# The input's transpose as a product with diag(1/rms), and tokens 256 to 511 first

## The chip, the core and the metric

The kernel runs on one core of one Trainium2 chip. A core has a matrix engine (TensorE, PE in the profile, with its weight loads as PEld), a vector engine (VectorE, DVE), a scalar engine (ScalarE, ACT), a general engine (GpSimd, POOL) and a queue engine that only issues transfers (SyncE, SP). Each works through its own list of instructions in order; semaphores tie the lists together. The metric is the time of one execution in microseconds on the device.

## What is computed

One layer over 512 tokens of width 2048, with 16 learned meta tokens ahead of them. The opening that the change touches is the first two lines of the layer: the norm, and the projection by `w_in`.

```python
def rms_norm(x, gain):
    y = x * lax.rsqrt(jnp.mean(x * x, axis=-1, keepdims=True) + EPS)
    return y * gain

def hybrid_layer(x, ...):                     # x: meta tokens, then tokens
    h = rms_norm(x, norm_g)
    proj = h @ w_in                           # 2048 x 12368
    q_a, k_a, v_a, z_a, q_i, k_i, w_i, q_b, f_b, i_b, z_b, gates = split(proj)
    o_a = dsa_attention(...)                  # indexer scores, top-128 keys, attention
    o_b = hgrn2_chunkwise(...)                # gated recurrence in chunks of 64
    y = stack([o_a * silu(z_a), rms_norm(o_b) * silu(z_b)])
    p = einsum('btnc,ncd->btnd', y, w_branch)
    return x + sum(sigmoid(gates) * p, axis=2) @ w_out
```

All data are float32.

## The kernel before

**Layout.** The projections need h with channels on partitions, in 16 tiles of 128 channels (`kt` 0 to 15) by 528 tokens: columns 0 to 15 are the meta tokens, then four blocks of 128 tokens, numbered 0 to 3. x comes with tokens on partitions, four pieces of 512 channels for each block (`load_x`, tiles `x` in the profile; `xm` for the meta tokens, two tiles of 1024 channels). The meta tokens and blocks 0 and 1 make half 0 (272 columns), blocks 2 and 3 half 1 (256 columns).

**Precision.** Every large product runs on the fast type fp32r in three matmuls. An operand is held as a rounded part and a remainder: `hH` and `hL` for the input, `eh`/`el` or `wh`/`wl` for weights out of the loaded `raw` tiles. ACT writes the rounded part, DVE (for some early weights POOL) the remainder. `mm3` issues high by high, high by low and low by high.

**The opening, step by step.** `norm_x(b)` is a generator: sums of squares of two pieces on ACT and two on DVE (two yields), then the mean and the power -1/2 on POOL (one yield; the factor 1/rms lies in `st[b][:, 6]`), then four scalings of x in place by that factor on DVE, one for each piece, with a yield behind each. `prep(half, kt)` transposes the scaled pieces of its blocks for tile kt into one PSUM bank `px` (`E.tr`, line 102), and then ACT (`hH`) and DVE (`hL`) read the bank with the norm's gain as scale. The main loop runs half 0 and then half 1; in each it goes over kt, first calls `prep` two tiles ahead, then issues six projection matmuls into `pg`: three for 80 columns of the indexer's keys and weights, three for the first 128 columns of its queries. `FIRST` says in which order the norm's steps of the first blocks are written out before the loop, `NEXT` at which (half, kt) the other steps stand, `SPLITS` where weight chunks are split. `fill` issues transposes of the identity into a spare bank `pw`: 33 before the first `prep`, and four in each of the first three steps.

**Transfers.** SP issues, in this order, x of block 0, meta, x of block 1, four weight chunks, x of blocks 2 and 3, further weight chunks. The x tiles are slots of a pool and go back to it behind their last transpose; meta lies in two weight buffers.

**Behind the opening.** Classifying jobs follow (512-column matmuls `pg`: the indexer's queries, then four gate pieces; `jobs[2:]`), then pairs of column blocks by a Strassen scheme with seven products (`px`, `py`, `pz`, `pv`, `pw` from `hH`, `hL` and the sums `tT`). The sums are made by `tops_task` on DVE and ACT while the classifying jobs run; `place_t3` then overwrites half of `hH`/`hL` with one of them. Indexer scores, top-k (`topk_task`: on DVE, 16 rounds of maximum and replace for each of four blocks of queries), the mask tables, HGRN and attention are tasks (generators) too.

**What sets the order.** The program is written out by a planner on the host. `Core` keeps a modelled clock for each engine. `pump(limit)` lets tasks take a step when their inputs are due and the modelled DVE and ACT clocks are less than `limit` ahead of PE's. `finish(t)` takes steps of all tasks without a limit until t is done. At the last classifying job (`ji == nclass`) `finish(t_task[0])` is called, so that `tops_task` is written out whole before the job's matmuls. Tiles that find too few free slots (`hold`) are stored to memory (`held`) and fetched again.

Of the kernel before, what the change touches and what calls it, by code (L numbers as in the profile page):

```python
# [8 lines left out]
F32 = mybir.dt.float32  # L9
# [9 lines left out]
NM = 16  # L19
# [10 lines left out]
KQ = (144, 272, 400, 528)  # L30
WAIT = object()

FIRST = ((0, 2), ("m", 2), (0, 1), ("m", 1), (1, 3), (0, 1), ("m", 1), (1, 1))
NEXT = {(0, 0): (1,), (0, 2): (0, "m", 1), (0, 5): (0, "m", 1), (0, 6): (2,), (0, 7): (2,), (0, 8): (3,),
        (0, 9): (2, 3), (0, 10): (2, 3), (0, 11): (3,), (0, 13): (3,), (0, 15): (2, 3), (1, 2): (2, 3),
        (1, 6): (2,)}
SPLITS = {(0, 3): 2, (0, 4): 3, (1, 9): 4, (1, 12): 5}
LAT = 180.0
SAME = {"pe": 0.0, "act": 60.0, "dve": 125.0, "pool": 60.0}
MARGIN = 300.0  # L40
NZA = 4
FILL = 4
NSLOT = 71
ORDER = (1, 0)
NC_, ND_ = 1, 0
# [143 lines left out]
def hybrid_kernel(ctx, tc, x, meta, vecs, w_in, rows, w_branch, w_out,  # L189
# [15 lines left out]
    class Task:  # L205
# [3 lines left out]
        def step(self):  # L209
            try:  # L210
                r = next(self.gen)
            except StopIteration:
                self.done = True
                tasks.remove(self)
                return True
            if r is WAIT:
                return False
            self.t = r or 0.0
            return True
# [21 lines left out]
    def finish(t):  # L241
        z = 0
        while not t.done:
# [9 lines left out]
            else:  # L253
                any(u.step() for u in list(tasks)) or stuck("fin")

    need = [2]

    def bank(name):
# [15 lines left out]
    def slots(name, n=1, dt=F32):  # L274
        return [S.get(name, dt) for _ in range(n)]
# [5 lines left out]
    def ready(*aps):  # L281
        return max(E.ac.get(a.tensor.name, (0.0, ""))[0] for a in aps) + LAT

    X = {}
    blocks = [("m", NM, 0)] + [(b, 128, NM + 128 * b) for b in range(4)]

    def load_x(b, q):
        X[b] = slots("x", 4)
        for c in range(4):
            q.dma_start(X[b][c][:, :512], x[0, 128 * b:128 * b + 128, 512 * c:512 * c + 512])  # L290

# [1 line left out]
    E.dve([mhalf], [], 8, lambda v: v.memset(mhalf, -0.5))  # L293
    warm = cp.tile([128, 1], F32, name="warm")
    E.act(warm, mhalf[:, 0:1], AF.Square)
    load_x(0, nc.sync)
    ident = cp.tile([128, 128], F32, name="ident")
    nc.gpsimd.dma_start(ident, ident_d)
    vrow = cp.tile([35, 128], F32, name="vrow")
    nc.gpsimd.dma_start(vrow, vecs)  # L300
    X["m"] = []
    for c in range(2):
        s = wp.tile([128, 1024], F32, name=f"xm{c}", tag=f"wh{c}")
        nc.sync.dma_start(s[:NM, :], meta[:, 1024 * c:1024 * c + 1024])
        X["m"] += [s[:, 0:512], s[:, 512:1024]]
    load_x(1, nc.sync)
    RB = cp.tile([128, 192], F32, name="RB")
    tabA = cp.tile([128, 5, 64], F32, name="tabA")
    tabI = cp.tile([128, 5, 32], F32, name="tabI")
# [79 lines left out]
    def split_upto(i):  # L389
        while state["split"] <= min(i, len(preps_) - 1):  # L390
            k = state["split"]
            ch = preps_[k]
            if "pair" in ch:
                prep_op(k, ch)
            else:
                split_chunk(k, ch)
            state["split"] += 1
# [100 lines left out]

    st = {b: cp.tile([128, 8], F32, name=f"st{b}") for b, _, _ in blocks}
    junk = slots("junk", 2)  # L500

    def norm_x(b):
        p = NM if b == "m" else 128
        for c in range(4):
            xs, ac = X[b][c][:p, :512], st[b][:p, c:c + 1]
            if c % 2:
                E.dve([junk[c % 2], st[b]], [xs], 512, lambda v: v.scalar_tensor_tensor(
                    junk[c % 2][:p, :512], xs, 1.0, xs, op0=OP.mult, op1=OP.mult, accum_out=ac))
            else:
                E.act(junk[c % 2][:p, :512], xs, AF.Square, accum_out=ac)  # L510
            if c % 2:
                yield
        E.red(st[b][:p, 4:5], st[b][:p, 0:4])
        E.ts(st[b][:p, 5:6], st[b][:p, 4:5], 1.0 / D, EPS, OP.mult, OP.add)
        E.ptt(st[b][:p, 6:7], st[b][:p, 5:6], mhalf[:p, 0:1], OP.pow)
        yield
        for c in range(4):
            xs = X[b][c][:p, :512]
            E.ts(xs, xs, st[b][:p, 6:7], None, OP.mult)
            yield  # L520

    hH, hL = [], []

    def prep(half, kt):
        if half == 0:
            hH.append(slot("hH", F32R))
            hL.append(slot("hL", F32R))
        bs = ((("m", 0, 1)), (2, 3))[half]
        pb = B1.get("px")
        o = 0  # L530
        for b in bs:
            p = NM if b == "m" else 128
            E.tr(pb[:, o:o + p], X[b][kt // 4][:p, 128 * (kt % 4):128 * (kt % 4) + 128], ident[:p, :p])
            o += p
        c = slice(272 * half, 272 * half + o)
        g = cvec[:, kt:kt + 1]
        E.act(hH[kt][:, c], pb[:, :o], AF.Copy, scale=g)
        E.stt(hL[kt][:, c], pb[:, :o], g, hH[kt][:, c].bitcast(F32), OP.mult, OP.subtract)
        B1.put(pb)
        if kt % 4 == 3:  # L540
            S.put(*[X[b][kt // 4] for b in bs if b != "m"])
# [1261 lines left out]
    stream[1], stream[2] = stream[2], stream[1]  # L1803
    preps_[1], preps_[2] = preps_[2], preps_[1]
    load_upto(3)
    load_x(2, nc.sync)
    load_x(3, nc.sync)
    load_upto(NRAW - 1)
    pb = B1.get("pc")
    E.tr(pb[:, :35], vrow, ident[:35, :35])  # L1810
# [10 lines left out]
        for _ in range(n):  # L1821
            next(gens[b], None)

    for b, n in FIRST[:4]:
        step(b, n)
    E.act(cvec, pb[:, :35], AF.Copy)
    B1.put(pb)
    for b, n in FIRST[4:]:
        step(b, n)
    split_upto(0)  # L1830
    prep(0, 0)
    split_upto(1)
    step(0)
    step("m")
    kb, qb = B2.get("pg"), B1.get("pg")
    preps = iter([(i, kt) for i in range(2) for kt in range(KT)][1:])

    def prep_next():
        p = next(preps, None)
# [1 line left out]
            prep(*p)  # L1841

    prep_next()
    for half in range(2):
        n = (272, 256)[half]
        for kt in range(KT):
            prep_next()
            if half == 0 and kt < 3:
                fill(FILL)
            elif half == 0 and kt == 3:  # L1850
                B1.put(pw)
            for ji in range(2):
                if ji == 0:
                    c = slice(272 * half, 272 * half + n)
                    o = kb[:80, half, :n]
                else:
                    c = slice(16 + 256 * half, 272 + 256 * half)
                    o = qb[:, 256 * half:256 * half + 256]
                mm3(o, jobs[ji].chunks[kt // 8], kt % 8, kt, hH[kt][:, c], hL[kt][:, c], kt == 0, kt == KT - 1)
            for b in NEXT.get((half, kt), ()):  # L1860
                step(b)
            if (half, kt) in SPLITS:
                split_upto(SPLITS[half, kt])
            if (half, kt) == (1, 8):
                load_consts()
    jobs[0].done(kb)
    jobs[1].done(qb)
    S.put(*junk, *early)
    for k in E.clk:
        E.clk[k] = max(E.clk[k], E.clk["pe"]) + (2500.0 if k in ("dve", "act") else 0.0)  # L1870
    npair, late = 0, []
# [1 line left out]
    for ji, job in enumerate(jobs[2:], 3):  # L1873
        need[0] = 1 + jobs[ji].meta if ji < len(jobs) else 0
        if job.pre:
            job.pre()
        if job.req:
            job.req()
        if job.kind == "pair":
            npair += 1  # L1880
            last = npair == npairs
            run_pair(job, jobs[ji] if isinstance(jobs[ji], Pair) else None, late, last)
            continue
        if job.kind == "br" and isinstance(job, Pair):
            finish(t_y)
            run_br(job, jobs[ji] if isinstance(jobs[ji], Pair) else None, job.c0 // 256, job.unit)
            continue
        if job.kind == "out":
            if ji - 1 == first_out:
                OB.extend(B1.get("po") for _ in range(6))  # L1890
                OB.append(B2.get("po")[:, 0])
                load_xq(0)
            nxt = jobs[ji] if ji < len(jobs) else None
            run_out(job, nxt)
            continue
        z = 0
        while len(B1.free) < 1 + job.meta:
            z += 1
            if z > 3000:
                stuck("job")  # L1900
            pump(1e9)
            if len(B1.free) < 1 + job.meta:
                E.clk["pe"] += 200
        if job.meta:
            b = [B1.get("pg"), B1.get("pg")]
            parts = [(b[c][:, :264], slice(264 * c, 264 * c + 264)) for c in range(2)]
        else:
            b = B1.get("pg")
            parts = [(b[:job.ncols, :], slice(16, 528) if job.kind == "in" else slice(0, 512))]
        if ji == nclass:  # L1910
            finish(t_task[0])
        for ch in job.chunks:
            split_upto(ch["prep"] + 2)
            flush()
            for kk_ in range(ch["nk"]):
                kt = ch["k0"] + kk_
                if job.kind == "in":
                    mh, ml = hH[kt], hL[kt]
                else:
                    mh, ml = yH[job.n, kt], yL[job.n, kt]  # L1920
                for o, c in parts:
                    mm3(o, ch, kk_, kt, mh[:, c], ml[:, c], kt == 0, kt == job.kts - 1)
                pump(500.0 if ji == nclass else 3000.0)
            if ji == nclass and ch["k0"] == 0:
                place_t3(0)
                place_t3(4)
        job.done(b)
# [72 lines left out]
```

## Time and profile before

| | us |
|---|---|
| median of 3 runs (lowest, highest) | 1530.59 (1528.6, 1531.83) |
| the profiled execution, its own time | 1529.07 |
| span of that profile | 1527.3 |
| first matmul on PE | 7.91 |
| first projection matmul (`pg`) | 15.98 |
| first 512-column projection matmul | 51.33 |
| first Strassen matmul | 195.55 |

A row of the timeline reads: start, duration, engine, line of the kernel, operation, result<-operands by the names in the kernel, shapes, count. A count x2 or more merges instructions that follow each other, and the duration then runs from the first start to the last end. In square brackets stands how long the engine sat idle before, and what ended that. A matmul's duration holds its way through the array, so matmuls overlap; what one costs is read from the distance of starts. Groups give busy time, mean nanoseconds of one, and the idle time before them. A stretch's row gives its bounds and length, then busy time and count of PE, PEld, DVE, ACT and POOL, the granted clock, the share of the DMA engines and GB/s.

### The profile page before, as it was taken

Reading aid. Unit: us, or ns where it says so; the run is one execution under the profiler, and the core shown is the slowest. Engines: PE = TensorE matmul, PEld = TensorE weight load, DVE = VectorE, ACT = ScalarE, POOL = GpSimd, SP = SyncE. Lnnn points to the kernel's source line nnn. Section 1 sums busy time; section 2 is a strip of 40 time slices with the busy share of each in tenths; the row PEclk is TensorE's granted clock in tenths of the full one; section 3 lists DMA queues with packets and bytes.
Section 4 is the critical chain, followed back from the end, with each engine's and each line's share of the span. In section 5 each row is a group of like instructions: output and inputs, shape, how many; then the busy total and the mean of one; then the engine's idle time right before and its main releaser. Section 6 shows DMA issues by size and latency. Waiting matters only on the chain.

```text
span 1527.3 us, 31296 instructions
## 1 busy us (share of the span) xinstructions
PE 1500.9 (98%) x12756; PEld 1435.2 (94%) x12756; DVE 1201.0 (79%) x2013; ACT 712.5 (47%) x1079; POOL 165.9 (11%) x180
## 2 busy tenths in 40 slices
PE   7999999999999999999999999999999999999998
PEld 6888889999999999999999999999999799989998
DVE  6699899999977787787768768768756768898765
ACT  5565444444434444434554554554454544444342
POOL 2100010010001001011101101101010000002221
PEclk9999999999999999999999999999999999999999
DMA  9323448766666585758677677676678767748883
GB/s 266 83 70 83 110 103 196 187 168 166 162 172 164 148 190 137 185 131 198 142 192 181 156 192 180 161 191 166 164 203 195 228 188 188 212 123 217 214 214 90
DMA packets 300288, 256.50 MB, mean 168 GB/s; under 512 B 11828, under 2 KB 262208, under 8 KB 300144
## 3 DMA queue, kind: packets, MB, share of 16 engines
q1 hardware_dynamic: 271392, 177.44, 40.0%
q0 software_dynamic: 15616, 56.71, 21.3%
q10 hardware_dynamic: 13136, 20.35, 4.2%
q8 instruction: 100, 1.64, 0.5%
q14 instruction: 44, 0.36, 0.1%
HBM read 169.11 MB, written 28.73 MB: 130 GB/s over the span
## 4 chain that ended last, share of the span: by engine, by line
PE 86%; DVE 8%; DMA 2%; issue 2%; ACT 2%; ACTq 0%; SPq 0%; POOL 0%; DVEq 0%
PE pz L96 16%; PE px L96 16%; PE pg L98 12%; PE po L96 10%; PE pv L96 8%; PE pw L96 8%; PE py L96 8%; DVE wl L112 2%; PE phl L98 1%; PE pov L96 1%; PE psc L98 1%; PE plg L98 1%; PE pho L98 1%; ACT wh L106 1%; DVE tk L697 1%
## 5 line engine op out<-in xcount | busy, mean ns | idle before, releaser
L106 ACT ACTIVATE wh<-raw 128x1024 fp32r<-128x1024 f32 x416 | 440.1, 1059 | 557.7 <-PE pz L96 148.9
L112 DVE TENSOR_TENSOR wl<-raw,wh 128x1024 fp32r<-128x1024 f32 x414 | 508.3, 1228 | 148.1 <-ACT wh L106 144.7
L121 POOL DMA_DIRECT2D raw<-raw x108 | 95.0, 993 | 969.0 <-DVE raw L112 678.3
L96 PE MATMUL px<-hH,wh 128*128 128x272 f32 (+1 forms) x672 | 194.6, 290 | 1.3 <-ACT p L106 1.3
L96 PE MATMUL px<-hL,wh 128*128 128x272 f32 (+1 forms) x672 | 192.1, 286 | 0.0
L96 PE MATMUL px<-hH,wl 128*128 128x272 f32 (+1 forms) x672 | 192.1, 286 | 0.0
L96 PE MATMUL po<-wh,mh 128*128 128x256 f32 x896 | 158.5, 281 | 0.5 <-DVE xq L112 0.5
L96 PEld LDWEIGHTS po<-wh,mh 128*128 128x128 f32 x896 | 137.3, 189 | 0.8 <-DVE xq L112 0.7
L112 DVE TENSOR_TENSOR raw<-raw,raw 128x1024 f32<-128x1024 f32 x108 | 132.0, 1222 | 1.8
L96 PEld LDWEIGHTS px<-hH,wh 128*128 128x128 f32 x672 | 126.9, 189 | 2.1 <-ACT p L106 1.6
L96 PEld LDWEIGHTS px<-hL,wh 128*128 128x128 f32 x672 | 126.9, 189 | 0.0
L96 PEld LDWEIGHTS px<-hH,wl 128*128 128x128 f32 x672 | 126.8, 189 | 0.0
L96 PE MATMUL pw<-tT,wh 128*128 128x256 f32 x672 | 126.4, 287 | 0.0
L96 PE MATMUL po<-wl,mh 128*128 128x256 f32 x448 | 125.7, 280 | 0.0
L96 PE MATMUL pv<-tT,wh 128*128 128x256 f32 x672 | 125.1, 285 | 0.0
L96 PE MATMUL pz<-tT,wh 128*128 128x256 f32 x672 | 124.3, 284 | 0.2 <-ACT wh L106 0.2
L96 PEld LDWEIGHTS pz<-tT,wh 128*128 128x128 f32 x672 | 103.2, 189 | 0.9 <-ACT wh L106 0.4
L96 PEld LDWEIGHTS pv<-tT,wh 128*128 128x128 f32 x672 | 103.0, 189 | 0.5
L96 PEld LDWEIGHTS pw<-tT,wh 128*128 128x128 f32 x672 | 103.1, 189 | 0.2
L96 PE MATMUL pz<-hH,wh 128*128 128x256 f32 x336 | 97.3, 289 | 2.9 <-DVE r L112 2.9
L96 PE MATMUL py<-hH,wl 128*128 128x256 f32 x336 | 94.8, 282 | 1.9 <-DVE wl L112 1.9
L96 PE MATMUL py<-hH,wh 128*128 128x256 f32 x336 | 95.9, 286 | 0.0
(349 smaller groups left out, 3582.9 us busy)
## 6 DMA issues: line engine op xcount, KB each, us to landing
raw<-in_w_in_dram SPq DMA_DIRECT2D x192, 512.0 KB, 6.1
raw<-raw POOLq DMA_DIRECT2D x108, 512.0 KB, 6.0
raw<-in_w_branch_dram SPq DMA_DIRECT2D x32, 512.0 KB, 6.3
raw<-in_w_out_dram SPq DMA_DIRECT2D x32, 512.0 KB, 6.5
gd<-r SPq DMA_DIRECT2D x32, 256.0 KB, 2.0
gate<-gd SPq DMA_DIRECT2D x32, 256.0 KB, 6.2
held<-r SPq DMA_DIRECT2D x19, 264.0 KB, 4.0
held<-r SPq DMA_DIRECT2D x18, 256.0 KB, 2.0
```

The lines of the kernel that those rows point to most:

```text
L96: self.nc.tensor.matmul(out, lhsT, rhs, start=start, stop=stop, skip_group_check=True)
L98: self.nc.tensor.matmul(out, lhsT, rhs, start=start, stop=stop)
L106: self.nc.scalar.activation(out, in_, f, **kw)
L112: self.nc.vector.tensor_tensor(out, a, b, op=op)
L121: self.nc.gpsimd.dma_start(out, a, accum_op=OP.add)
L697: e = E.dve([w], [src, m8], kq, lambda v: v.match_replace(w, m8, src, NEG))
```

## The change

The norm's factor is no longer multiplied into x. `norm_x` ends with one instruction that multiplies the identity by the block's factors, which gives the diagonal matrix `DG[b]` (128x128, for meta 16x16, in one new slot `dg`), and `prep` multiplies the unscaled x by it: the transpose `E.tr` becomes an ordinary float32 matmul with x as stationary and `DG[b]` as moving operand. The halves change places: the loop runs half 1 first (blocks 2 and 3, no meta), then half 0 (meta, 0, 1). Block 2 and 3 are loaded first; meta and blocks 0 and 1 behind the first four weight chunks. `FIRST` and `NEXT` follow. At the last classifying job `alone` takes the place of `finish`: it steps only `tops_task`, and lets other tasks step, up to 1500 ns ahead (`FLOOD`), only where that one is blocked.

```diff
-FIRST = ((0, 2), ("m", 2), (0, 1), ("m", 1), (1, 3), (0, 1), ("m", 1), (1, 1))
-NEXT = {(0, 0): (1,), (0, 2): (0, "m", 1), (0, 5): (0, "m", 1), (0, 6): (2,), (0, 7): (2,), (0, 8): (3,),
...
+FIRST = ((2, 3), (3, 2), (2, 1), (3, 2))
+NEXT = {(0, 4): ("m",), (0, 5): ("m",), (0, 6): (0,), (0, 7): (0,), (0, 8): (1,), (0, 9): (0, 1), (0, 10): (0, 1), (0, 11): (1, "m"),
...
+FLOOD = 1500.0
...
+    def alone(t):
+
+        z = 0
+        while not t.done:
+            z += 1
+            if z > 3000:
+                stuck("alone")
+            if t.t > E.clk["pe"]:
+                E.clk["pe"] = t.t
+            elif not t.step():
+                pump(FLOOD)
+                E.clk["pe"] += 200
...
-    load_x(0, nc.sync)
+    load_x(2, nc.sync)
...
-    X["m"] = []
-    for c in range(2):
-        s = wp.tile([128, 1024], F32, name=f"xm{c}", tag=f"wh{c}")
-        nc.sync.dma_start(s[:NM, :], meta[:, 1024 * c:1024 * c + 1024])
-        X["m"] += [s[:, 0:512], s[:, 512:1024]]
-    load_x(1, nc.sync)
+    load_x(3, nc.sync)
...
+    dg, DG = slot("dg"), {}
...
-        for c in range(4):
-            xs = X[b][c][:p, :512]
-            E.ts(xs, xs, st[b][:p, 6:7], None, OP.mult)
-            yield
+        DG[b] = dg[:p, 512:512 + NM] if b == "m" else dg[:, 128 * b:128 * b + 128]
+        E.ts(DG[b], ident[:p, :p], st[b][:p, 6:7], None, OP.mult)
+        yield
...
-        if half == 0:
+        if len(hH) <= kt:
...
-            E.tr(pb[:, o:o + p], X[b][kt // 4][:p, 128 * (kt % 4):128 * (kt % 4) + 128], ident[:p, :p])
+            E.mm(pb[:, o:o + p], X[b][kt // 4][:p, 128 * (kt % 4):128 * (kt % 4) + 128], DG[b], True, True)
...
     load_upto(3)
-    load_x(2, nc.sync)
-    load_x(3, nc.sync)
+    X["m"] = []
+    for c in range(2):
+        s = wp.tile([128, 1024], F32, name=f"xm{c}", tag=("wh0", "wl0")[c])
+        nc.sync.dma_start(s[:NM, :], meta_t[:, 1024 * c:1024 * c + 1024])
+        X["m"] += [s[:, 0:512], s[:, 512:1024]]
+    load_x(0, nc.sync)
+    load_x(1, nc.sync)
     load_upto(NRAW - 1)
...
-    prep(0, 0)
+    prep(1, 0)
     split_upto(1)
-    step(0)
-    step("m")
     kb, qb = B2.get("pg"), B1.get("pg")
-    preps = iter([(i, kt) for i in range(2) for kt in range(KT)][1:])
+    preps = iter([(i, kt) for i in (1, 0) for kt in range(KT)][1:])
...
-    for half in range(2):
+    for turn, half in enumerate((1, 0)):
...
-    S.put(*junk, *early)
+    S.put(*junk, *early, dg)
...
         if ji == nclass:
-            finish(t_task[0])
+            alone(t_task[0])
```

How this moves instructions shows at three places.

On PE, behind the 33 warming transposes, before the change (`px` is the bank that `prep` fills, `x_73` a piece of block 0, `x_89` of block 1, `xm` meta, `pw` the fillers):

```order
L102 MATMUL pw_196<-ident 128x128 x33
L102 MATMUL px_267<-ident,xm_85 128x16
L102 MATMUL px_267<-ident,x_73 128x128
L102 MATMUL px_267<-ident,x_89 128x128
...
L102 MATMUL px_299<-ident,x_89 128x128
L102 MATMUL pw_196<-ident 128x128 x4
L98 MATMUL pg_287<-hH_265,eh_255 80x272
```

The same place with the change (`x_73` is now a piece of block 2, `x_85` of block 3):

```order
L102 MATMUL pw_197<-ident 128x128 x33
L98 MATMUL px_260<-dg_109,x_73 128x128
L98 MATMUL px_260<-dg_109,x_85 128x128
...
L98 MATMUL px_288<-dg_109,x_85 128x128
L102 MATMUL pw_197<-ident 128x128 x4
L98 MATMUL pg_277<-hH_258,eh_248 80x256
```

The transposes have become products of x and `dg`, and in the first turn two stand for a tile and not three; the six projection matmuls of a step are as many as before.

On SP, the first transfers from the fourth on, before the change:

```order
L290 DMA x_76<-in_x_dram 128x512
L304 DMA xm_85<-in_meta_dram 16x1024
L304 DMA xm_87<-in_meta_dram 16x1024
L290 DMA x_89<-in_x_dram 128x512
L290 DMA x_90<-in_x_dram 128x512
L290 DMA x_91<-in_x_dram 128x512
L290 DMA x_92<-in_x_dram 128x512
L381 DMA raw_166<-in_w_in_dram 128x8x80
```

And with it:

```order
L303 DMA x_76<-in_x_dram 128x512
L303 DMA x_85<-in_x_dram 128x512
L303 DMA x_86<-in_x_dram 128x512
L303 DMA x_87<-in_x_dram 128x512
L303 DMA x_88<-in_x_dram 128x512
L389 DMA raw_163<-in_w_in_dram 128x8x80
```

The second block of x and the first weights move ahead by the two transfers of meta.

On DVE, at the last classifying job, before the change (`tr` and `tT` are steps of `tops_task`, MAX and MATCH_REPLACE a round of top-k, `masks` the mask tables, `wl` the remainder of the first Strassen weight):

```order
L112 TENSOR_TENSOR tr_2077<-tr_2075,tr_2076 128x256
L324 CAST masks<-mf_2037 128x256
L696 MAX m_120<-tk_1998 128x8
L697 MATCH_REPLACE tk_1998<-m_120,tk_1998 128x528
L112 TENSOR_TENSOR tT_2117<-tr_2076,tT_2116 128x512
L112 TENSOR_TENSOR tT_2118<-tr_2077,tT_2118 128x256
L324 CAST masks<-mf_2037 128x256
L696 MAX m_120<-tk_1998 128x8
L697 MATCH_REPLACE tk_1998<-m_120,tk_1998 128x528
L112 TENSOR_TENSOR wl_2127<-raw_1732,wh_2126 128x1024
```

And with it:

```order
L112 TENSOR_TENSOR tr_2063<-tr_2061,tr_2062 128x256
L112 TENSOR_TENSOR tT_2099<-tr_2062,tT_2098 128x512
L112 TENSOR_TENSOR tT_2100<-tr_2063,tT_2100 128x256
L112 TENSOR_TENSOR wl_2106<-raw_1718,wh_2105 128x1024
L332 CAST masks<-mf_2023 128x256
```

Two rounds of top-k and two casts have left this stretch. From the start of top-k to the next weight remainder (`wl_2177` before, `wl_2158` after, behind the eight instructions of `place_t3`) eight rounds and five casts stand before the change, six and four with it; the rest stands later. Two more things move with the planner's clocks: 41 tiles are stored as `held` in place of 37, and the steps of HGRN stand up to 150 projection matmuls later. From the attention's end on, PE's list is the same.

More of the change, by code (lines that the diff above doesn't have):

```diff
@@ L31 @@
 WAIT = object()
-FIRST = ((0, 2), ("m", 2), (0, 1), ("m", 1), (1, 3), (0, 1), ("m", 1), (1, 1))
-NEXT = {(0, 0): (1,), (0, 2): (0, "m", 1), (0, 5): (0, "m", 1), (0, 6): (2,), (0, 7): (2,), (0, 8): (3,),
-        (0, 9): (2, 3), (0, 10): (2, 3), (0, 11): (3,), (0, 13): (3,), (0, 15): (2, 3), (1, 2): (2, 3),
-        (1, 6): (2,)}
+FIRST = ((2, 3), (3, 2), (2, 1), (3, 2))
+NEXT = {(0, 4): ("m",), (0, 5): ("m",), (0, 6): (0,), (0, 7): (0,), (0, 8): (1,), (0, 9): (0, 1), (0, 10): (0, 1), (0, 11): (1, "m"),
+        (0, 12): ("m",)}
 SPLITS = {(0, 3): 2, (0, 4): 3, (1, 9): 4, (1, 12): 5}
@@ L282, in ready @@
         return max(E.ac.get(a.tensor.name, (0.0, ""))[0] for a in aps) + LAT
-    X = {}
+    X, meta_t = {}, meta
     blocks = [("m", NM, 0)] + [(b, 128, NM + 128 * b) for b in range(4)]
@@ L1822, in step @@
             next(gens[b], None)
-    for b, n in FIRST[:4]:
+    for b, n in FIRST[:2]:
         step(b, n)
@@ L1827, in hybrid_kernel @@
     B1.put(pb)
-    for b, n in FIRST[4:]:
+    for b, n in FIRST[2:]:
         step(b, n)
     split_upto(0)
-    prep(0, 0)
+    prep(1, 0)
     split_upto(1)
-    step(0)
-    step("m")
     kb, qb = B2.get("pg"), B1.get("pg")
-    preps = iter([(i, kt) for i in range(2) for kt in range(KT)][1:])
+    preps = iter([(i, kt) for i in (1, 0) for kt in range(KT)][1:])
     def prep_next():
@@ L1847, in hybrid_kernel @@
             prep_next()
-            if half == 0 and kt < 3:
+            if turn == 0 and kt < 3:
                 fill(FILL)
-            elif half == 0 and kt == 3:
+            elif turn == 0 and kt == 3:
                 B1.put(pw)
@@ L1859, in hybrid_kernel @@
                 mm3(o, jobs[ji].chunks[kt // 8], kt % 8, kt, hH[kt][:, c], hL[kt][:, c], kt == 0, kt == KT - 1)
-            for b in NEXT.get((half, kt), ()):
+            for b in NEXT.get((turn, kt), ()):
                 step(b)
-            if (half, kt) in SPLITS:
-                split_upto(SPLITS[half, kt])
-            if (half, kt) == (1, 8):
+            if (turn, kt) in SPLITS:
+                split_upto(SPLITS[turn, kt])
+            if (turn, kt) == (1, 8):
                 load_consts()
```

## The prediction

> **What bounds the kernel now.** First the page's busy times and the chain that ended last:
>
> ```profile
> PE 1500.9 (98%) x12756; PEld 1435.2 (94%) x12756; DVE 1201.0 (79%) x2013; ACT 712.5 (47%) x1079; POOL 165.9 (11%) x180
> PE 86%; DVE 8%; DMA 2%; issue 2%; ACT 2%; ACTq 0%; SPq 0%; POOL 0%; DVEq 0%
> ```
>
> TensorE (PE) is busy 1500.9 of 1527.3 us and is 86% of the chain. So work added to PE is added to the time, unless it lands where PE now waits. Next the table by stretches for the opening (us from the start; the second number after the length is PE's busy time):
>
> ```profile
> 20.00:30.00 10.00, 9.91 (x72) 8.41 (x70) 8.05 (x18) 7.33 (x19) 4.40 (x4) 1.00 1.13 313
> 30.00:40.00 10.00, 10.00 (x81) 9.49 (x82) 8.16 (x24) 4.76 (x12) 1.49 (x2) 1.00 0.55 160
> 40.00:60.00 20.00, 20.00 (x139) 18.20 (x138) 12.37 (x25) 12.12 (x24) 6.26 (x4) 1.00 0.29 79
> ```
>
> From 20 us on PE is full there, at granted clock 1.00, while VectorE (DVE) has a fifth of its time free. Last the list of what PE waited for, at the start and between 150 and 230 us:
>
> ```profile
> PE pc L102 <- DMA vrow<-in_vecs_dram: 7.9, 1, 7.9
> PE py L96 <- DVE wl L112: 1.9, 1, 1.9
> PE pz L96 <- DVE r L112: 0.9, 1, 0.9
> PE pv L96 <- DVE wl L112: 0.2, 1, 0.2
> ```
>
> The 7.9 us are the wait for the first input, which the change leaves. The other three, together 3.0 us, lie just behind the place where the new loop `alone` works.
>
> **The change part by part.** *The product in place of the transpose.* Per step of the opening PE issues the transposes of a later step and six projection matmuls. These rows are the starts of two steps with the 16-row meta block xm and one pair of transposes behind it, of two steps without it, of two that transpose nothing, and of the first matmul behind the opening:
>
> ```profile
> 32.42 0.23 PE L102 MATMUL px<-ident,xm 16*128 16x16 f32 x1
> 33.67 0.23 PE L102 MATMUL px<-ident,xm 16*128 16x16 f32 x1
> 33.84 0.44 PE L102 MATMUL px<-ident,x 128*128 128x128 f32 x2
> 37.67 0.38 PE L102 MATMUL px<-ident,x 128*128 128x128 f32 x2
> 38.60 0.38 PE L102 MATMUL px<-ident,x 128*128 128x128 f32 x2
> 49.74 0.28 PE L98 MATMUL pg<-hH,eh 128*80 128x256 f32 x1
> 50.45 0.28 PE L98 MATMUL pg<-hH,eh 128*80 128x256 f32 x1
> 51.33 0.39 PE L98 MATMUL pg<-hH,wh 128*128 128x512 f32 x1
> ```
>
> A step with two transposes takes 38.60 - 37.67 = 0.93 us, six matmuls alone 50.45 - 49.74 = 0.71. So a transpose costs (0.93 - 0.71) / 2 = 0.11 us (0.108 with the next digit), one record each (x2 for two). The change makes it an ordinary float32 matmul of 128x128 by 128x128. Such matmuls run later in this trace; here are the first and the last of eight in a row (x2 for one), and a float32 product of 16 rows with what follows it:
>
> ```profile
> 307.67 0.38 PE L98 MATMUL pho<-hk,attn 128*128 128x128 f32 x2
> 309.23 0.39 PE L98 MATMUL pho<-S,QA 128*128 128x128 f32 x2
> 302.58 0.48 PE L98 MATMUL phs<-mt 16*128 16x128 f32 x2
> 303.00 0.94 PE L98 MATMUL phs<-hk,kd 128*128 128x128 f32 x6
> ```
>
> Seven products take 309.23 - 307.67 = 1.56 us, 0.223 each, in two records. So each of the 64 x products costs 0.223 - 0.108 = 0.115 more: **+7.4 us**. The operands and shapes are the same, so this is a price and not a bound.
>
> The 16 xm products are not in the trace. Below, the second record could hide wholly: 0. Above, two records with 128 moving columns take 303.00 - 302.58 = 0.42, one xm record 33.84 - 33.67 = 0.17: 0.25 more. I take the middle, 0.12, since xm moves 16 columns, not 128, but loads the same 128 columns of weights: **+1.9 us** (0 to 4).
>
> Here a rule of the Trainium skill bears. Its page Perfetto Trace Analysis, section Transposes, says that a logical transpose should use the transpose and not a standard matmul; TensorE: Matmul & The Clock Gate, section Terms, calls transpose mode four times faster for FP32. By four times 0.108 the 64 products would cost 64 x 0.324 = 20.7 us more instead of 7.4; the rows above show a factor of 2.07 here, and the sum uses the rows.
>
> *The scaling that goes.* 16 scalings of x and four of xm leave DVE, five short ones of 128 or 16 columns come:
>
> ```profile
> L128 DVE TENSOR_SCALAR x<-x,st 128x512 f32<-128x512 f32 x16 | 7.6, 485 | 0.4 <-POOL st L116 0.3
> 18.34 0.35 PE L98 MATMUL pg<-hL,eh 128*80 128x272 f32 x1 [0.30 <-DVE hL L135]
> L106 ACT ACTIVATE junk<-x 128x512 f32<-128x512 f32 x8 | 5.0, 625 | 4.6 <-DMA x<-in_x_dram 4.6
> L106 ACT ACTIVATE eh<-raw 128x512 fp32r<-128x512 f32 x4 | 2.3, 619 | 0.0
> L106 ACT ACTIVATE hH<-px,cvec 128x256 fp32r<-128x256 f32 x16 | 7.6, 473 | 6.0 <-PE px L102 6.0
> ```
>
> That is over 7.6 us off DVE, but beside a full PE; PE's recorded wait for hL in the opening is 0.30. What is late next is ScalarE (ACT): its sums of squares (0.63 each, plus the read-out of the sum) for m, 0 and 1 and its weight copies (0.62) now fall between the copies hH (0.47) of the first turn, three kinds in steps of 0.71 + 2 x 0.223 = 1.16 us. So I take nothing saved, with -0.9 to +1 as its range.
>
> *The start.* The end of the warming transposes, the first wait of the weight load, the fillers, the first projection, and the meta sum, the last sum and the scaling of block 1 on DVE:
>
> ```profile
> 8.13 5.66 PE L102 MATMUL pw<-ident 128*128 128x128 f32 x33
> 13.84 0.13 PEld L102 LDWEIGHTS px<-ident,xm 16*128 16x128 f32 x1 [0.29 <-DVE xm L128]
> 15.62 0.60 PE L102 MATMUL pw<-ident 128*128 128x128 f32 x4
> 15.98 0.37 PE L98 MATMUL pg<-hH,eh 128*80 128x272 f32 x1
> 10.02 0.68 DVE L507 SCALAR_TENSOR_TENSOR junk<-xm 16x512 f32<-16x512 f32 x1
> 12.45 0.08 DVE L507 DVE_READ_ACCUMULATOR junk<-x 128x1 f32 x1
> 13.86 0.49 DVE L128 TENSOR_SCALAR x<-x,st 128x512 f32<-128x512 f32 x1
> ```
>
> PE is free at 13.84 - 0.29 = 13.55 and not before, because the 33 warming transposes stay. From the last sum (12.45) to the scaled block (14.35) DVE and POOL need 1.9; without two meta sums of 0.68 ahead and with a narrower scaling, the factors are there near 12.6, so the fillers become the bound. Six products (1.34) and four fillers (4 x 0.11) put the first projection at about 15.4: **-0.6 us**. If block 3's transfers share their bandwidth with the weights, now issued before meta, it can be +0.3; with the short wait above gone too, -1.5 in all.
>
> *The place of `alone`.* On DVE, behind the last projection of the classifying jobs, before the change (mask cast, one round of top-k from its maximum to the next instruction, the eight hL, and the weight remainder that PE waits for):
>
> ```profile
> 195.28 0.28 DVE L324 CAST masks<-mf 128x256 uint8<-128x256 f32 x1
> 195.48 0.70 DVE L696 MAX8 m<-tk 128x8 f32<-128x528 f32 x1
> 196.91 2.76 DVE L112 TENSOR_TENSOR hL<-t,hH 128x256 fp32r<-128x256 f32 x8
> 199.58 1.22 DVE L112 TENSOR_TENSOR wl<-raw,wh 128x1024 fp32r<-128x1024 f32 x1
> ```
>
> A round takes 196.91 - 195.48 = 1.43, a cast 0.20 of queue (195.48 - 195.28). Eight rounds and five casts stand before that remainder now; six and four in the changed order. 2 x 1.43 + 0.2 = 3.06 us less ahead of it: PE's 1.9 and 0.2 go, and then 0.9 + 2.1 - 3.06 is below zero, so the wait for r goes too: **-3.0 us** at most. The two rounds come later, beside the Strassen pairs (the third rival takes the case that they do not fit). Zero is the other end, if a transfer and not DVE's queue ends these waits; the row naming DVE is why I take the near end.
>
> *What else moves.* Four more tiles go out to memory and back, and HGRN's steps stand up to 150 projection matmuls later:
>
> ```profile
> held<-r SPq DMA_DIRECT2D x19, 264.0 KB, 4.0
> PE pka L102 <- DMA xk<-held: 0.6, 1, 0.6
> ```
>
> Such a store lands in 4 us, beside a PE that is full; of all fetches one costs PE 0.6 now. I count nothing, 0 to +1.5.
>
> **The sum.** 7.4 + 1.9 + 0 - 0.6 - 3.0 = +5.7 us. On the profiled execution (1529.07 us, of which the span is 1527.3) that is 1534.8. That execution lies 1.5 below the median of the runs, 1530.59, so the forecast for a median is 1530.59 + 5.7 = **1536.3 us**.
>
> **The rivals.**
>
> *Faster: the second record hides.* If, between fp32r matmuls, the product's second record ran in the shadow of the next weight load, the 64 and the 16 products would cost as the transposes do. The point is the step of the first turn: at 0.93 us it decides for this, at 1.16 against. Then start and queue remain: -0.6 - 0.9 - 3.0 = -4.5, or 1526.1. Against it stands that pho's records lie 0.11 apart one after the other. Chance 0.06.
>
> *No change: everything else pays in full.* xm free, the short waits of the opening gone: 7.4 - 1.5 - 3.0 = +2.9, or 1533.5, just within 0.2% (3.1 us, about what a measurement of this kernel tells from no change). For it: all three gains are real rows; against it: ACT takes DVE's place in the first turn. Chance 0.20.
>
> *Dearer: the waits near 200 us only move.* The stretch behind them, in the columns of the stretches above with DVE fifth (busy us and count):
>
> ```profile
> 230.00:300.00 70.00, 70.00 (x735) 68.78 (x734) 68.23 (x127) 29.69 (x37) 5.16 (x6) 1.00 0.80 191
> ```
>
> DVE is busy 68.23 of these 70 us, and the two delayed rounds must fit there. If PE then waits for DVE as it did before, the 3.0 is not won: +8.7, or 1539.3; with xm at its upper end 1541.4. Against it: ahead of every later remainder less DVE work stands than before. Chance 0.20.
>
> *Four times.* If float32 operands of the opening made a product cost four transposes, 0.43, the 64 would add 20.7 in place of 7.4: +19.0, or 1549.6. The two records and 0.223 of pho speak against it. The factor is the one that the Trainium skill states (TensorE: Matmul & The Clock Gate, Terms). Chance 0.02.
>
> **How the numbers follow.** The forecast has the remaining 0.52. Its own parts run from 1533.8 (xm nearly free) to 1539 (xm near its upper end, trips not hidden). The range takes in that, most of "no change" and most of "dearer": 1532.5 to 1540.5. Outside are the faster rival, the four times, and the outer thirds of the two others, some 0.2. Faster by over 0.2%: 0.07. Within: 0.20. Slower: 0.73.
>
> **What would show it.** In the changed profile the step of the first turn should be 1.16 us and of the second, 33.67 - 32.42 = 1.25 now, 1.25 + 0.23 + 0.12 = 1.60; px should have 160 records in the opening, and the 512-column projections, which start at 51.33 now, should start near 60. The rows `py <- wl` and `pz <- r` near 205 should be gone. I am wrong if the first turn's step is 0.93, if PE waits for px's copies over 2 us in all, or if waits of over 3 us appear between 230 and 760 us, where the order of the HGRN steps is new.

## The result and the profile after

The changed kernel takes 1544.81 us (median of 5 runs, 1544.32 to 1547.77), the kernel before, run beside it, 1530.52 (5 runs, 1527.5 to 1531.83): 14.3 us more, ratio 1.0103 with a 95% interval of 1.0088 to 1.0118. The forecast was 1536.3, and the range ended at 1540.5. The direction was right and the size was not: +14.3 where +5.7 was forecast. The profiles compared below lie 15.7 us apart, since the profiled execution of before is 1.5 below its median; the account of the parts is that of the 15.7.

First the page of the changed kernel, busy times and the chain that ended last:

```profile
PE 1513.3 (98%) x12836; PEld 1446.7 (94%) x12836; DVE 1194.0 (77%) x1998; ACT 713.2 (46%) x1079; POOL 165.7 (11%) x180
PE 85%; DVE 6%; DMA 4%; ACT 2%; issue 2%; SPq 1%; ACTq 0%; DVEq 0%
```

PE has 80 records more, the second records of the 80 products, and is busy 12.4 us longer in a span that is 15.7 longer (1543.0). The share of transfers in the chain has doubled, from 2% to 4%; 1% of it is `v<-held`, fetches that PE didn't wait for before. The stretches of the opening and the one behind `alone`:

```profile
20.00:30.00 10.00, 9.95 (x87) 9.71 (x86) 8.75 (x26) 8.44 (x25) 5.83 (x5) 1.00 1.11 307
30.00:40.00 10.00, 9.48 (x71) 8.62 (x70) 3.92 (x12) 2.79 (x7) 1.09 (x2) 1.00 0.55 161
40.00:60.00 20.00, 20.00 (x147) 18.25 (x146) 6.01 (x12) 7.70 (x14) 4.05 (x2) 1.00 0.10 27
230.00:300.00 70.00, 69.51 (x727) 68.38 (x725) 66.89 (x117) 30.73 (x39) 5.87 (x8) 1.00 0.70 171
```

PE is as full in the opening as it was, but for 0.52 us at 32 us, where the first xm product starts late. From 40 to 60 us DVE is busy 6.01 us, where it was 12.37 before (in part because the opening fills that stretch longer now); PE gains nothing by that, since it waits for nobody there. From 230 to 300 us, where PE had no gap, it has 0.49 now.

Next the steps of the opening, from the timeline of PE: two steps of the first turn (two x products and six projections), two of the second (with an xm product ahead), and the first 512-column matmul.

```profile
18.59 0.61 PE L98 MATMUL px<-dg,x 128*128 128x128 f32 x4
19.74 0.61 PE L98 MATMUL px<-dg,x 128*128 128x128 f32 x4
40.59 0.39 PE L98 MATMUL px<-dg,xm 16*128 16x16 f32 x2
42.28 0.39 PE L98 MATMUL px<-dg,xm 16*128 16x16 f32 x2
60.48 0.40 PE L98 MATMUL pg<-hH,wh 128*128 128x512 f32 x1
```

The first turn's step is 19.74 - 18.59 = 1.15, as forecast (1.16). The second turn's is 42.28 - 40.59 = 1.69, not 1.60. The opening ends 60.48 - 51.33 = 9.15 later; forecast were 7.4 + 1.9 - 0.6 = 8.7. Then the list of what PE waited for:

```profile
PE phl L102 <- DMA v<-held: 3.5, 3, 2.2
PE pz L96 <- DVE r L112: 2.3, 4, 0.9
...
PE ppt L102 <- ACT lg L106: 1.6, 2, 1.4
PE pov L96 <- ACT pT L106: 1.4, 4, 0.5
...
PE py L96 <- DVE wl L112: 0.7, 1, 0.7
```

Of the waits near 200 us that were to vanish, `py <- wl` is down from 1.9 to 0.7, and `pz <- r` at 225 us is still 0.9. New are waits of HGRN (`phl`, the first matmul of a head) for its v, which had been stored to memory, and of attention (`ppt`) for its logits. The longest one in the timeline, the issue of the fetch and the matmul that waited, with the stretch between them and 2 us of it:

```profile
518.23 0.33 ACTq L813 DMA_DIRECT2D v<-held  x1
526.40 0.28 PE L102 MATMUL phl<-ident,v 128*16 128x128 f32 x1 [2.22 <-DMA v<-held]
518.20:526.40 8.20, 5.98 (x49) 5.77 (x48) 5.40 (x7) 3.99 (x5) 0.00 (x0) 1.00 1.03 239
520.00:522.00 2.00, 2.00 (x19) 2.00 (x18) 0.53 (x1) 0.76 (x1) 0.00 (x0) 1.00 1.07 254
```

The planner counts 4 us for a fetch (`fetch`: PE's clock + 4000). This one took about 8 from issue to use, beside weight loads and a store that filled the DMA engines (share 1.03 over the whole, 1.07 in the 2 us). The list of transfers (count, KB, median us from issue to landing) has eight such fetches, before it had four, here the one of before first:

```profile
v<-held ACTq DMA_DIRECT2D x4, 264.0 KB, 5.4
v<-held ACTq DMA_DIRECT2D x8, 264.0 KB, 4.9
```

The order in which projection matmuls follow each other is the same in all kernels here; only the tasks between them move. So the same matmul can be looked up in each timeline. This table gives how much later than in the profile of before it starts, in us, for the changed kernel and the experiments below:

| matmul (its start before) | after | e1 | e2 | e3 | e4 | e9 | e11 |
|---|---|---|---|---|---|---|---|
| first projection (15.98) | -1.6 | -1.9 | 0.3 | 0.5 | -0.9 | -1.0 | -0.1 |
| second turn (36.88) | -0.6 | -1.0 | 0.3 | 5.9 | 0.2 | -1.0 | -0.1 |
| first 512-column (51.33) | 9.2 | 8.7 | 0.3 | 8.6 | 4.3 | -1.0 | -0.1 |
| ahead of the waits (190.92) | 9.5 | 9.1 | 0.3 | 8.9 | 4.6 | -1.0 | -0.1 |
| behind them (229.53) | 8.6 | 10.4 | -1.8 | 10.4 | 2.5 | -4.7 | 0.0 |
| HGRN, middle (518.53) | 8.3 | 11.1 | -1.9 | 11.9 | 3.1 | -1.3 | 3.9 |
| attention begun (810.10) | 14.8 | 11.4 | 4.6 | 12.2 | 10.1 | -1.3 | 11.1 |
| last projection (1522.41) | 15.7 | 12.0 | 5.0 | 13.2 | 12.4 | -1.9 | 10.7 |

At the start, profiles of one and the same opening (e2, e9, e11) lie up to 1.3 apart, so the first rows are good to about 1 us; the differences down a column are better than that up to 810 us (e9, with PE's order of before, keeps its distance within 0.1 from 518 to 810 us), and less good behind it (e10, with the same order, drifts by 2.5 there). The row at 518 us compares only kernels of one order: with `alone` 184 fewer matmuls of tasks stand ahead of it than before, in e11 48 fewer; at the other rows the counts are equal. The column "after" is the account of the 15.7: opening +9.2, up to 190 us +0.3, at the place of `alone` -0.9, between 230 and 810 us **+6.3**, behind that +0.9. Between 230 and 810 us PE issues the same tasks in both kernels (the matmuls differ only in whether an operand had been stored); its waits there are 6.3 against 2.0 before. Here are PE's lists for that part alone, two rows of before and then five of the changed kernel:

```profile
PE pz L96 <- DVE r L112: 1.4, 1, 1.4
PE phd L98 <- ACT hk L106: 0.6, 2, 0.3
PE phl L102 <- DMA v<-held: 3.5, 3, 2.2
PE ppt L102 <- ACT lg L106: 1.6, 2, 1.4
PE pov L96 <- ACT pT L106: 0.5, 1, 0.5
PE pz L96 <- DVE r L112: 0.5, 1, 0.5
PE phs L98 <- ACT mt L106: 0.2, 1, 0.2
```

So 4.3 of the 6.3 are waits, and 1.9 lie in steps that are a little longer without a named wait; the granted clock is 1.00 there in both.

### The profile page after: what moved, and what is told of

Read it like the earlier page. It is cut to its first block, busy times and chain, and to the rows that moved or that the text cites. A ratio compares the mean times of both kernels' runs of the same rounds, so it can differ in the third digit from the quotient of the medians.

```text
span 1543.0 us, 31447 instructions
## 1 busy us (share of the span) xinstructions
PE 1513.3 (98%) x12836; PEld 1446.7 (94%) x12836; DVE 1194.0 (77%) x1998; ACT 713.2 (46%) x1079; POOL 165.7 (11%) x180
## 4 chain that ended last, share of the span: by engine, by line
PE 85%; DVE 6%; DMA 4%; ACT 2%; issue 2%; SPq 1%; ACTq 0%; DVEq 0%
PE px L96 15%; PE pz L96 15%; PE pg L98 13%; PE po L96 10%; PE py L96 7%; PE pv L96 7%; PE pw L96 7%; DVE wl L112 2%; PE phl L98 1%; PE psc L98 1%; DMA v<-held 1%; ACT wh L106 1%; PE px L98 1%; PE plg L98 1%; PE pov L96 1%
```

## The experiments

Each ran beside the kernel before, whose median was 1529.2 to 1529.3 in all three sets. From the first 512-column matmul on, PE's rows stand in one of two orders in before, after and e1 to e4: that of `finish` or that of `alone`, whatever the opening is.

**e1: the changed kernel with `finish`.**

```diff
-            alone(t_task[0])
+            finish(t_task[0])
```

> The changed kernel with one line undone: `finish` again in place of `alone`. From the first 512-column projection on, PE's instructions then stand in the order of before, to the last one. Before is 1530.5, the changed kernel 1544.8. Theory A (the two halves of the change add up: the opening costs about 9.2, and `alone` costs about 5.3, because its order brings PE into waits for v<-held and ppt<-lg between 400 and 770 us): 1539.5 to 1540.5, the distance to before stays at 9 from 60 us to the end, no v<-held wait. Rival B (`alone` is worth its forecast gain, and the 6 us come from the later end of the opening, which shifts every transfer and step behind it): 1546 to 1548, and the distance to before grows by some 6 between 230 and 830 us.

1541.61, ratio 1.0086 (1.0072 to 1.0099): +12.3. Nearer to A than to B, but above A's range. The growth between 230 and 810 us is gone (1.0 in place of 6.3) and so are the v waits; B is out. What A lacked is 1.3 us near 200, read from PE's list of waits:

```profile
PE py L96 <- DVE wl L112: 3.1, 1, 3.1
```

It was 1.9 before, with the same order on DVE. Where it comes from stands in ACT's timeline 30 us earlier, here in before and in e3, and DVE's part in the stretch behind it (of before):

```profile
169.25 0.58 ACT L106 ACTIVATE rl<-psc 128x144 f32<-128x144 f32 x2 [5.21 <-DMA zd<-zs]
179.55 0.58 ACT L106 ACTIVATE rl<-psc 128x144 f32<-128x144 f32 x2 [6.58 <-DMA zd<-zs]
185.00:202.00 17.00, 15.11 (x82) 12.91 (x81) 16.76 (x41) 7.64 (x16) 0.00 (x0) 1.00 0.19 62
```

ACT stands behind a store, and DVE behind ACT; DVE is then busy 16.76 of 17 us up to 202 and makes up for nothing. SP issues the store at 164.57 in before and at 173.48 in e3, 8.9 later, as all of PE is; ACT goes on 4.7 and 6.1 behind that, and the remainder that PE waits for starts 10.3 later (209.88 against 199.58), as ACT does. ACT's wait is 6.47 to 6.58 in the three kernels with products and 5.15 to 5.35 in those with transposes (before, e2, e4). Why the store takes longer there was not tested.

In e1, but not in e3, the long wait is followed by a stretch at half the clock:

```profile
211.70:215.10 3.40, 3.40 (x18) 3.40 (x18) 3.33 (x6) 0.00 (x0) 0.00 (x0) 0.50 0.00 0
```

It adds 1.5, which PE gets back: the waits `pv <- wl` and `pz <- r` behind it are gone in e1. So 1.3 remains here, about the 1.4 of e3.

**e2: the kernel before with `alone`** (its function and `FLOOD`, and the one line of e1 the other way round).

> The kernel before with `alone` in place of `finish` and nothing else: the old opening, and from the first 512-column projection on the order of the changed kernel. Theory A: 1530.5 - 0.95 (the shorter wait py<-wl near 200) + 6.3 = 1535.5 to 1536.5, with v<-held waits of 2 to 4 us in all. Rival B: 1527.5 to 1529.6, no such waits.

1533.66, ratio 1.0033 (1.0021 to 1.0044): +4.4. A's mechanism, but 1.8 below A's range; B is out here too. `alone` wins 2.1 near 200 us and loses 6.4 between 230 and 810, without any change to the opening. PE's list of waits shows the same rows as the changed kernel's:

```profile
PE phl L103 <- DMA v<-held: 4.1, 4, 2.9
PE ppt L103 <- ACT lg L107: 1.6, 2, 1.4
```

**e3: the kernel before with the products** (`dg`, one scaling of the identity for each block, `E.mm` in `prep`; the halves, `FIRST`, `NEXT` and `finish` as before).

> The kernel before with the factors in the transposing matrix and nothing else: old order of the halves, old order of everything behind the opening. Theory A (a product costs 0.115 more than a transpose, an xm product about 0.2 more): steps of the first turn 1.25 -> 1.69, of the second 0.93 -> 1.16, in all 16 x 0.44 + 16 x 0.23 = 10.7, less 0.3 to 0.5 at the start: 1540.2 to 1541.2. Rival C (part of the opening's price in the changed kernel comes from its order, with ACT behind in the turn with three copies): 1537 to 1539. Were the scalings that leave DVE worth something later, it would be below both.

1543.38, ratio 1.0096 (1.0081 to 1.0112): +14.1, above A's range. Its steps, from the timeline, are A's: 24.98 - 23.30 = 1.68.

```profile
23.30 0.39 PE L98 MATMUL px<-dg,xm 16*128 16x16 f32 x2
24.98 0.39 PE L98 MATMUL px<-dg,xm 16*128 16x16 f32 x2
```

The opening costs 8.6 and not 10.2 to 10.4: the products of three tiles stand ahead of the first projection and delay it by 0.5 only, not by three times 0.44, and steps that are up to 0.5 too long in before (1.0 us in all) are not so here. To that come the 1.4 at `py <- wl` as in e1, a v wait of 0.9 and another 2.3 spread to the end. The order of the halves plays no part in the price of a product: C is out for that, though its range and A's both lie below the measured time.

**e4: the changed kernel with transposes of a scaled x** (four scalings again in `norm_x`, `E.tr` in `prep`; three more steps for each block in `FIRST` and `NEXT`; the slot `dg` stays taken).

> The changed kernel (tokens 256 to 511 first, meta in the second half, `alone`) with transposes of a scaled x again; the slot of the factors stays taken, and from the first 512-column projection on the order is that of the changed kernel. Theory A: the products cost 64 x 0.115 + 16 x 0.2 = 10.6, so 1544.8 - 10.6 = 1534.2, and 1534 to 1535.5 with the longer scaling at the start; steps 0.93 in the first turn, 1.25 in the second. Rival C (the order of the halves carries some of the 9.2): 1536 to 1539.

1538.29, ratio 1.0068 (1.0055 to 1.008): +9.0, in C's range for another reason than C's. The steps are 0.93 and 1.25 as A says, but PE waits 4.2 us at five places up to 34 us, for a scaled x or xm and for hL that stands behind scalings and sums on DVE; the one named `issue` is the longest, and the scaling of xm just ahead of it ends at 33.70 + 0.47 = 34.17:

```profile
PE pg L98 <- DVE hL L135: 1.8, 3, 1.1
PE px L102 <- issue: 1.5, 1, 1.5
PE px L102 <- DVE x L128: 0.9, 1, 0.9
33.70 0.47 DVE L128 TENSOR_SCALAR xm<-xm,stm 16x512 f32<-16x512 f32 x1
34.28 0.20 PE L102 MATMUL px<-ident,xm 16*128 16x16 f32 x1 [1.52 <-issue]
```

So in this order, with the scalings at these places, the products are not 10.6 dearer than the transposes but 9.2 - 4.3 = 4.9. Whether better places would save the 4.2 was not tried.

**e5 to e7: `alone`, with the planner nudged against the new waits** (all on the kernel of e2).

```diff
-        E.wr[s.tensor.name] = (E.clk["pe"] + 4000.0, "dma")
+        E.wr[s.tensor.name] = (E.clk["pe"] + (6000.0 if name == "v" else 4000.0), "dma")   # e5
+        E.wr[s.tensor.name] = (E.clk["pe"] + 9000.0, "dma")                                # e6
-ROOMY = 8
+ROOMY = 6                                                                                  # e7
```

> The kernel before with `alone`, and the planner's time for the fetch of a spilled v 6 us in place of 4 (the fetches of e2 landed later than the plan had it, and PE waited 4.0 us for them in the profile). Theory A1 (what `alone` costs behind 230 us is these waits and the three for lg and pT, nearly nothing else): 1533.7 - 4 = 1529.2 to 1530.5, and no row of phl waiting for v. Rival D (any new order of the HGRN steps costs some 4 to 7 against the order of before, the waits only change their names): 1532 to 1537, with other waits in sum as large.

> The kernel before with `alone`, and every fetch of a spilled tile planned at 9 us in place of 4. Theory A1: as e5, 1529 to 1531, no wait for a held tile between 230 and 760 us. Rival D: 1532 to 1537.

> The kernel before with `alone`, and a tile spilled only below 6 free slots in place of 8: 30 spills in place of 41, three fetches of v in place of eight. Theory A1: fewer fetches on the path: 1528.5 to 1530.5. Rival D: 1532 to 1537; a wait for room in place of a wait for a fetch would show as gaps of PE with DVE or ACT as releaser.

e5 1547.35 (ratio 1.0116, 1.01 to 1.0132), e6 1576.26 (1.0307, 1.0292 to 1.0322), e7 1547.0 (1.0124, 1.0099 to 1.015): all far above A1, and above D's range too. In e5 the v waits fall from 4.1 to 0.9, nearly as A1 said, but others come: 2.0 for top-k, 2.7 for another stored operand, 5.3 for r at 1183 us. In e7 one of three fetches of v still costs 3.9, and the waits for r are 5.5 in all (2.9 before). In e6 PE waits 0.6 in all between 230 and 810 us, against 2.0 before. What that plan put off stands behind the last pair, where no projections cover it. The stretches of e6, the second of them that one:

```profile
230.00:810.00 580.00, 579.40 (x6017) 566.92 (x6016) 465.58 (x803) 242.53 (x324) 50.73 (x58) 1.00 0.71 173
1160.00:1250.00 90.00, 57.85 (x276) 47.45 (x274) 44.35 (x109) 36.08 (x74) 4.69 (x7) 0.73 0.41 131
```

PE is busy 579.4 of 580 us in the first, and 57.85 of 90 in the second. A stretch without waits is no gain if its work is only moved to where nothing hides it.

**e8, e11, e12: the kernel before, `finish` and all, with the planner nudged.**

```diff
-        E.wr[s.tensor.name] = (E.clk["pe"] + 4000.0, "dma")
+        E.wr[s.tensor.name] = (E.clk["pe"] + 7000.0, "dma")   # e8
+        E.wr[s.tensor.name] = (E.clk["pe"] + 4100.0, "dma")   # e12
-MARGIN = 300.0
+MARGIN = 320.0                                                # e11
```

> The kernel before, `finish` and all, with the fetches planned at 7 us in place of 4: the HGRN steps stand in a third order without `alone` having a part in it (41 spills in place of 37). Theory A1: before has no wait for a held tile in this stretch, so nothing is won and little lost: 1529 to 1531. Rival D (the order of before happens to hold few waits, and another costs 3 to 6 whatever made it): 1532 to 1536.

> The kernel before, `finish` and all, with the planner's reserve ahead of a step at 320 ns in place of 300: from 230 us on PE's order differs in about as many rows as with `alone`, and 38 tiles are spilled in place of 37. Theory D (the order of before holds few waits, and what another costs is a matter of chance, nothing that `alone` does in particular): 3 to 25 slower, 1532 to 1554. Rival A1 (`alone` does a harm of its own, by delaying top-k and with it the HGRN steps): within 2 of before, 1527.5 to 1531.5.

> The kernel before with fetches planned at 4.1 us in place of 4.0, another small nudge that changes about as many rows of PE's order as `alone` does. Theory D: 3 to 25 slower, 1532 to 1554. Rival A1: within 2 of before, 1527.5 to 1531.5.

e8 1551.39 (ratio 1.0153, 1.013 to 1.0177), e11 1541.92 (1.0091, 1.0077 to 1.0105), e12 1534.28 (1.0036, 1.0023 to 1.005): D in e11 and e12, and beyond D's range for this run in e8; A1 is out. A reserve of 320 ns in place of 300 costs 12.7 us, a fetch planned 0.1 us longer 5.1. In PE's list of waits in e11 the first of these rows is 2.7 where before and after have 0.6 and 0.7, and the second is in neither:

```profile
PE pka L102 <- DMA xk<-held: 2.7, 2, 2.1
PE phl L98 <- DVE QA L112: 2.4, 4, 1.3
```

e8 loses its time as e6 does: it is 10.4 us ahead of before at 810 us, and then 24.0 us pass between the last projection of the last pair and the next projection (0.1 in before, 60.1 in e6):

```profile
1184.00:1207.70 23.70, 12.13 (x46) 9.43 (x45) 9.11 (x26) 9.62 (x22) 0.00 (x0) 0.63 0.56 169
```

Seven orders other than that of before were run, four of them with `alone`; all are slower, by 4.4 to 47 us, and the one of `alone` itself is the cheapest (4.4, with e12 at 5.1).

**e9 and e10: the gain of `alone` without its order.** The plan of before is kept to the last row of PE; on DVE alone, the last two rounds of top-k and two mask casts that `finish` writes out are held back and written out behind the weight remainder (e9: later rounds stay behind by as much until the first query block is done; e10: they follow two remainders later).

```diff
+        if late and self.late is not None and self.skip < 0:
+            self.late.append(f)
+        else:
+            f(self.nc.vector)
...
+            E.late, E.skip = [], 6
             finish(t_task[0])
...
             split_upto(op["prep"] + 2)
+            E.drain(6)
```

(Of `drain`: e9 leaves six instructions waiting, e10 writes out up to six; at the classifying job's second weight chunk e10 writes out three.)

> The kernel before with its plan and PE's order left as they are to the last row; on DVE alone, two rounds of top-k and two casts of the masks are written out behind the weight remainder near 200 us in place of ahead of it, and the rounds behind them stay late by that much until the first query block is done. This is the gain of `alone` without its new order. Forecast's term: -3.0, 1526.3. Theory E (as in e2: py<-wl 1.9 and pv<-wl 0.2 go, pz<-r 0.9 stays): -2.1, 1527.2, and no growth behind 230 us. Rival F (DVE is full, the waits only move): 1529.0 to 1529.8, with pz<-r grown to some 3.

> As e9, but the two rounds and two casts are written out again two weight remainders later, ahead of the next r that PE waits for. Theory E says that what matters is the DVE work ahead of each remainder and r: py<-wl goes, but pz<-r near 216 grows from 0.9 to some 3, and the time is 1529.0 to 1529.8 (no change). Rival G (DVE has room between the remainder and r): 1527.2, pz<-r 0.9.

e9 1529.0, ratio 1.0001 (0.9992 to 1.001); e10 1529.4, ratio 1.0003 (0.9994 to 1.0012): no change, in F's range for e9 and E's for e10, though neither had the place of the waits. In e9 all three waits near 200 us go: the table shows -1.0 ahead of them and -4.7 behind, 3.8 won. F had them move to `pz <- r` at once; they come later: the table's line of HGRN has -1.3 again, 3.4 of the 3.8 are lost by 320 us, 2.2 of them in these waits, which before doesn't have:

```profile
239.50 0.39 PE L97 MATMUL py<-hH,wl 128*128 128x256 f32 x1 [1.12 <-DVE wl L113]
245.87 0.39 PE L97 MATMUL pv<-tT,wl 128*128 128x256 f32 x1 [0.27 <-DVE wl L113]
279.56 0.35 PE L97 MATMUL pz<-hH,wh 128*128 128x256 f32 x1 [0.85 <-DVE r L113]
```

In e10 PE waits 1.65 for a weight copy and 0.76 for a remainder at 206 to 208 us instead, not for r as E had it: the two rounds stand on DVE ahead of a sum of weights (`raw`), and the copy behind that. None of the twelve kernels is measurably faster than before.

## Why the forecast was short

*The 64 x products, +7.4:* right. A step without xm is 1.15 against 0.93, so a product costs 0.22, 0.11 more than a transpose: 64 x 0.11 = 7.0, or 7.4 with 0.115; 7.2 below. That is a factor of about 2. So the rivals *four times* (1549.6) and *the second record hides* (0.93) are out. The four of the page TensorE: Matmul & The Clock Gate in the Trainium skill, section Terms, does not show here.

*The 16 xm products, +1.9 of 0 to 4:* too small. The step with xm grew by 1.68 - 1.25 = 0.43 in the mean of the steps, of which two x products take 0.22; an xm product costs 0.21 more, in both orders of the halves: 16 x 0.21 = +3.4.

*Scaling and start, 0 and -0.6:* together they came out at 9.2 - 7.2 - 3.4 = -1.4. The first projection starts 1.6 earlier and not 0.6. The bound was as said: PE goes from the first warming transpose to the first projection without a gap. But it started 0.4 earlier, and the 33 transposes took 5.12 us in place of 5.66; in e9 and e11, which open as before does, they took 5.26 and 6.42, so this is luck of the profile. PE's only recorded wait of the opening behind that is 0.5; ACT did not become late. That the opening as a whole came out near the forecast, 9.2 for 8.7, is luck too: the xm products were 1.5 dearer, and scaling and start 0.8 cheaper.

*The place of `alone`, -3.0:* it is -0.9 in the changed kernel, and the step of the forecast holds two errors. Against `finish` in the same kernel the gain is 2.2 (the distance grows by 1.3 there in e1 and shrinks by 0.9 here), in e2 it is 2.1; `pz <- r` stays. And 1.3 of it pays for the store that lands later, which the forecast did not have. That PE does win all of the 3 when enough DVE work is put off, and pays nearly all of it back by 320 us, is e9: the rival *dearer* ("the waits near 200 us only move") had the mechanism.

*What else moves, 0 of 0 to +1.5:* **this is the step that failed.** "Such a store lands in 4 us, beside a PE that is full; of all fetches one costs PE 0.6 now. I count nothing". It measured +6.3, and e2 shows it without the new opening. The list of before has a second such row, `pva <- xv<-held` with 0.3, but that is not the point. The reasoning priced the additional stores and fetches one by one, as if the rest of the order stayed. But `alone` leaves two rounds of top-k to later, the planner's clocks then differ by some us, and everything that it writes out from 230 us on stands elsewhere: four more heads of HGRN fetch their v (waits of 3.5), and attention waits for its logits (1.6), while a wait of 1.4 for r, at 746 us in before, goes. The forecast's last sentence named the sign of it, waits of over 3 us between 230 and 760 us, without giving it a price. e8, e11 and e12 show that the price is not that of `alone` in particular. Before's order holds few waits and leaves nothing uncovered behind the last pair; each of the others lost some us by the one or the other. Why before's order is so good no run shows. The cheapest and the dearest change of plan differ by a factor of ten, and nothing here lets one say ahead which it will be.

So of the 10 us that the profile of the changed kernel (+15.7) lies above the sum of the forecast (+5.7), 6.3 are the new order, 2.1 the place of `alone`, 0.5 the opening, and 1.2 are spread over the rest. What stays open: the 1.9 of the 6.3 without a named wait, and why the store before 180 us lands later behind an opening with products. (The low end of the forecast's own parts does not come out of them: with xm free and the rest as summed they give 1534.4, not 1533.8.)

## What to carry to other kernels

Where a planner with modelled clocks writes the order, any edit ahead of it, even one that only shortens a queue, buys a new order of all that follows; price it by nudging the planner by a trifle and timing that before the edit is judged, because the spread (here 5 and 13 us for two trifles, 22 for fetches planned 3 us longer) may be larger than every term that was worked out. Look for it at two places: in the waits, and where work was put off until nothing covers it. To keep the gain of a moved instruction without the new order, move it below the plan, on its own engine, and look whether PE gets the time back or only waits later. A product in place of a transpose cost PE about twice as much per block here (0.22 against 0.11 us), so where PE is full it can only pay by the waits for the scaling that it saves.

## What the runs showed of the hardware

A step with an xm product is 1.69 - 1.15 = 0.54 longer than one without, more than two whole products of 128x128x128 (0.22 each) cost, though xm has 16 rows and moves 16 columns; the xm transposes of before added 1.25 - 0.93 = 0.32. Of the 0.54, by the starts of the timeline, 0.32 lie between the xm product and the next one, 0.11 in the two x products behind it (0.47 against 0.36) and 0.09 in the projections ahead of it: among large operands this small one was not cheap.

In e6, where PE is busy 57.85 of 90 us behind the last pair, the granted clock of that stretch is 0.73, against 1.00 in the stretch with 579.4 of 580; in e8 it is 0.63 with 12.13 of 23.7. There the work that was left uncovered also ran slower. Such a stretch also followed single waits: behind one of 3.10 us the clock of e1 is 0.50 for 3.4 us, and fp32r matmuls of 256 columns start 0.21 apart in place of 0.12. Not every wait has one: behind the same wait in e3, and behind the one of 2.22 at 526.40 in the changed kernel, the clock is 1.00. The warming transposes show the same two paces, 0.213 and then 0.109 us apart; the change came 2.7 us behind the first one in the changed kernel, 3.8 in before and 5.4 in e11.

A 264 KB fetch of v took 4.9 us in the median of the changed kernel and about 8 from issue to use in the longest, beside loads that kept the DMA engines at a share of 1.03.
